# A hybrid encoder layer on one core: even and odd sums in the FNet transform, input statistics from position-major copies, a spread filter network, and a second place for split activations

## Chip, cores and metric

The kernel runs on one core of a Trainium2 chip. The metric is the device time of one execution in microseconds (us); the time of a kernel is the median of its runs.

## What is computed

One layer of an encoder for 512 positions of width 2048. The input is normalised and projected; the columns of the projection feed four groups of 1024 channels and a gate. Each group has its own mixer, each result is RMS-normalised per group, multiplied by the SiLU of its gate, and a last product brings the 4096 channels back to 2048. The reference, cut:

```python
h = rms_norm(x, pre_g);  proj = h @ w_in
a, f, hy, q, gate = split(proj)
u = a_val * sigmoid(a_gate)                              # group A: convolution of 31 taps,
y_a = silu(layer_norm(depthwise_conv(u))) @ conv_pw_w + b  # layer norm, pointwise product
y_b = fft2(f).real @ fnet_w + fnet_b                     # group B: Fourier mixing
y_c = two gated long convolutions of hy                  # group C: Hyena; the filters come from
                                                         # a small network of sines over positions
y_m = attention(q, mem_n @ wk, mem_n @ wv)               # group M: 256 memory tokens
y = rms_norm(each group) * silu(gate)
out = x + rms_norm(y @ w_out, post_g)
```

## The kernel before

All numbers are float32. A product in full precision is made of three fast ones: `split` (L77 to L83) writes the rounded high part of a tile on ACT and the rest on DVE, and `mm3` (L111 to L114) multiplies high by high, low by high and high by low. A weight tile of 128x1024 arrives by one DMA on SP's queue (`load`, 3 buffers `raw`), is split (`wsplit`, 3 buffers `wh` and `wl`), and is consumed by TensorE (PE). `project` (L313) is one output tile of the big projection: 16 steps of 3 matmuls of 512 columns, 48 in all, into a PSUM tile `pf`. A generator that is given to it as `fill` is advanced four times within it.

The order in which the instructions stand on each engine is made by a scheduler from the program; it pulls splits and loads ahead of where they are written. Each engine, and SP's queue of DMAs, then runs its own list strictly in order.

The stages, in order of time:

- **Values loop** (L291 to L310): 16 steps, each loads a slice of `wv`, and every second step a pair of memory slices. Beside it, eight pairs of `xT`, the channel-major input, arrive; ACT squares them and the memory slices, and POOL adds the squares up in `xacc` and `macc` (L189 to L207).
- **Norm of the input**: 8 products with a column of ones (`column_sums`, L156) sum `xacc` over the partitions; `spread` (L147) brings the 512 factors to all partitions by four small products.
- **Keys loop** (L346 to L352): 16 steps with `wk`, matmuls of 256 columns; beside it the normalised input is formed and split into `hH` and `hL`.
- **Filter network** (L257 to L289), after the first of four early query projections: two matmuls (L273, L280) with a sine between them that takes DVE several steps.
- **Filters, then the Hyena group** with the first convolutions. The change does not touch them.
- **FNet group**: a product with `w_f` (folded over positions), then products with a cosine table `cg` and a sine table `sg` (L727 to L752) of 512 columns, small products with `cgx` (L740 to L744), the transform along positions, and `out_product` (L790 to L834), which runs as `fill` of projections.
- **Attention**, with gates and convolutions.
- **Layer norm of group A** (L941 to L973): the mean is subtracted (L952), the squares are summed in `vacc` by ACT and POOL (`group_square`, L480), then column sums, root, spread, and per channel tile a scaling, a SiLU and a split into `uH` and `uL`. Projections for the last gates run on PE meanwhile.
- **Pointwise product of group A**, its last gates, then `group_norm(0, ...)` (L503): column sums, spread, and for seven tiles a scaling (L500) and the product with an early gate (L998).
- **Last product** (rounds of L1027 on): 5 rounds over 32 slices of the mixed channels, group C first, then B, M and A. Activations are split into `jh` and `jl` (3 buffers each) in pool `wp4`, which is opened when the memory of pool `wp5` (`uH`, `uL`, `lnt`, and the early gates that reuse `uL`) has been given back, so it waits for the last reader of that memory.

## Time and profile before

| what | value |
|---|---|
| median of 3 runs | 1719.39 us (1713.63 to 1721.88) |
| profiled execution | 1716.29 us |
| its span, first to last instruction | 1714.5 us |
| PE busy | 1655.3 us, 97% |
| DVE busy | 1221.9 us, 71% |
| ACT busy | 813.6 us, 47% |
| POOL busy | 189.9 us, 11% |
| mean granted clock of TensorE | 0.987 of full speed |
| moved by DMA | 240.27 MB, mean 140 GB/s |

PE's busy share overlaps neighbouring matmuls, so it is read as where PE has work, not as speed. A matmul's row gives its length, some of which overlaps the next one; the pace is the length of a stretch without idle time over the count of matmuls in it. Names of tiles stand without buffer numbers. `<-` after a wait names what ended it.

### The profile page before, as it was taken

How to read it: one execution, taken by the hardware profiler on the slowest of the kernel's cores; microseconds unless marked ns; L12 is line 12 of the kernel's file. 1: busy time of each engine (PE TensorE's matmuls, PEld its weight loads, DVE VectorE, ACT ScalarE, POOL GpSimd, SP SyncE). 2: the span in 40 equal slices, each digit the busy share in tenths (PEclk: the TensorE clock that was granted, in tenths of full speed). 3: DMA queues.
4: the chain of work that ended last, by engine and by line, in shares of the span. 5: the costliest groups of instructions: out<-in, count | busy, mean ns of one | idle time of the engine just before them, and what ended most of it. 6: DMA issues, size and time to landing. Idle time of an engine off the chain costs nothing.

```text
span 1714.5 us, 21887 instructions
## 1 busy us (share of the span) xinstructions
PE 1655.3 (97%) x8201; PEld 1386.6 (81%) x8201; DVE 1221.9 (71%) x1835; ACT 813.6 (47%) x1185; POOL 189.9 (11%) x146
## 2 busy tenths in 40 slices
PE   7999999999999999999999999999999699999997
PEld 5997888887777778878888888888878588888876
DVE  7866987378797887989874979985562545454586
ACT  6645655344343443424344355445454434444564
POOL 5101422011020120100000020100212000000000
PEclk9999999999999999999999999999999899999999
DMA  8654545768576684623434334232123523222355
GB/s 290 227 185 156 160 139 158 218 155 176 136 171 150 146 181 126 137 93 106 134 105 133 105 124 153 81 111 86 62 98 109 193 98 102 93 101 98 128 203 179
DMA packets 87487, 240.27 MB, mean 140 GB/s; under 512 B 8915, under 2 KB 26579, under 8 KB 86869
## 3 DMA queue, kind: packets, MB, share of 16 engines
q1 hardware_dynamic: 80468, 213.70, 38.6%
q0 software_dynamic: 6912, 25.17, 7.9%
q8 instruction: 64, 1.05, 0.2%
q14 instruction: 43, 0.34, 0.1%
HBM read 220.21 MB, written 18.63 MB: 139 GB/s over the span
## 4 chain that ended last, share of the span: by engine, by line
PE 78%; DVE 14%; DMA 2%; issue 2%; ACT 2%; POOL 1%; SPq 0%; DVEq 0%; ACTq 0%; POOLq 0%
PE pf L114 14%; PE pf L112 14%; PE pf L113 14%; PE pg L113 11%; PE pg L112 11%; PE pg L114 11%; DVE y L525 5%; DVE wl L80 2%; DVE yc L629 1%; DMA raw<-in_wv_dram 1%; POOL vacc L485 1%; ACT wh L79 1%; DMA wl<-in_w_std_dram 1%; DVE y L630 1%; DVE pq L568 1%
## 5 line engine op out<-in xcount | busy, mean ns | idle before, releaser
L112 PE MATMUL pf<-hH,wh 128*128 128x512 f32 x1280 | 505.6, 395 | 0.0
L114 PE MATMUL pf<-hH,wl 128*128 128x512 f32 x1280 | 502.7, 393 | 0.3 <-DMA wl<-in_w_std_dram 0.3
L113 PE MATMUL pf<-hL,wh 128*128 128x512 f32 x1280 | 502.1, 392 | 0.0
L80 DVE TENSOR_TENSOR wl<-raw,wh 128x1024 fp32r<-128x1024 f32 (+1 forms) x240 | 304.0, 1269 | 151.6 <-ACT wh L79 151.0
L79 ACT ACTIVATE wh<-raw 128x1024 fp32r<-128x1024 f32 (+1 forms) x240 | 247.5, 1033 | 231.3 <-PE pf L113 140.8
L114 PEld LDWEIGHTS pf<-hH,wl 128*128 128x128 f32 x1280 | 241.5, 189 | 49.6 <-DMA wl<-in_w_std_dram 0.7
L113 PEld LDWEIGHTS pf<-hL,wh 128*128 128x128 f32 x1280 | 241.9, 189 | 46.9 <-issue 0.2
L112 PEld LDWEIGHTS pf<-hH,wh 128*128 128x128 f32 x1280 | 241.7, 189 | 46.9 <-issue 0.5
L80 DVE TENSOR_TENSOR jl<-y,jh 128x512 fp32r<-128x512 f32 (+1 forms) x154 | 91.3, 597 | 121.6 <-ACT jh L79 120.5
L79 ACT ACTIVATE jh<-y 128x512 fp32r<-128x512 f32 (+1 forms) x154 | 84.4, 550 | 178.6 <-PE pg L113 113.4
L112 PE MATMUL pg<-wh,jh 128*128 128x512 f32 x384 | 150.6, 392 | 11.2 <-ACT jh L79 11.2
L113 PE MATMUL pg<-wl,jh 128*128 128x512 f32 x384 | 150.5, 392 | 0.0
L114 PE MATMUL pg<-wh,jl 128*128 128x512 f32 x384 | 150.4, 392 | 0.0
L107 ACT ACTIVATE wh<-raw 128x1024 fp32r<-128x1024 f32 x48 | 51.0, 1061 | 99.8 <-PE pf L113 51.8
L525 DVE SCALAR_TENSOR_TENSOR y<-ubuf,par,y 128x512 f32<-128x512 f32 x120 | 93.0, 775 | 3.5 <-ACT y L523 1.5
L112 PEld LDWEIGHTS pg<-wh,jh 128*128 128x128 f32 x384 | 72.8, 189 | 26.6 <-ACT jh L79 11.5
L114 PEld LDWEIGHTS pg<-wh,jl 128*128 128x128 f32 x384 | 72.6, 189 | 15.2 <-DVE jl L80 0.2
L113 PEld LDWEIGHTS pg<-wl,jh 128*128 128x128 f32 x384 | 72.7, 189 | 15.1
L108 POOL DMA_DIRECT2D wl<-in_w_std_dram x48 | 41.7, 870 | 286.2 <-ACT wl L106 274.3
L106 ACT ACTIVATE wl<-raw 128x1024 fp32r<-128x1024 f32 x48 | 50.2, 1046 | 0.0
L525 DVE SCALAR_TENSOR_TENSOR y<-ub,par,y 128x512 f32<-128x512 f32 x60 | 46.4, 773 | 2.3 <-ACT y L523 1.1
L1016 POOL TENSOR_TENSOR xres<-xres,og 128x512 f32<-128x512 f32 x4 | 6.7, 1682 | 372.2 <-ACT og L1015 372.2
(380 smaller groups left out, 2916.8 us busy)
## 6 DMA issues: line engine op xcount, KB each, us to landing
raw<-in_w_std_dram SPq DMA_DIRECT2D x160, 512.0 KB, 4.2
raw<-in_wo_dram SPq DMA_DIRECT2D x77, 512.0 KB, 3.3
wl<-in_w_std_dram POOLq DMA_DIRECT2D x48, 512.0 KB, 7.8
raw<-in_wk_dram SPq DMA_DIRECT2D x16, 512.0 KB, 4.0
kd<-y SPq DMA_DIRECT2D x16, 512.0 KB, 4.9
y<-kd SPq DMA_DIRECT2D x32, 256.0 KB, 6.0
raw<-in_w_f_dram SPq DMA_DIRECT2D x16, 512.0 KB, 3.2
raw<-in_wv_dram SPq DMA_DIRECT2D x15, 512.0 KB, 5.2
```

Source lines behind the costliest of these rows:

```text
L79: act.activation(h, src, AF.Copy)
L80: dve.tensor_tensor(l, src, h, op=sub)
L106: act.activation(l, raw, AF.Copy, scale=-1.0)
L107: act.activation(h, raw, AF.Copy)
L108: pool.dma_start(l, src, accum_op=add)
L112: pe.matmul(ps, wh, xh, start=start, stop=False)
L113: pe.matmul(ps, wh, xl, start=False, stop=False)
L114: pe.matmul(ps, wl, xh, start=False, stop=stop)
L485: pool.tensor_tensor(acc, sqt, acc, op=add)
L525: dve.scalar_tensor_tensor(o, u[:, t:t + L], conv_w[:, ct, t:t + 1], o, op0=mul, op1=add)
L568: dve.tensor_tensor(pq[:, 0], z0, z1, op=add)
L629: dve.scalar_tensor_tensor(yv, pcv[:, h], cinv[:, o, ct:ct + 1], yv, op0=mul, op1=add)
```

## The change

Six edits.

1. **Start.** 24 products of a tile of ones with itself are put ahead of all other work on PE.
2. **Input statistics.** The sums of squares come from position-major copies: `squares` loads 128 positions (1 MB) and one ACT instruction squares and sums them into a column of `sums`. Four loads of `x` stand in the values loop (steps 5, 8, 10, 12), two of `mem` in the keys loop (steps 8, 11). The loads of `xT` move to the keys loop. The squares and POOL sums of before, and the column sums with ones, go.
3. **Filter network.** It becomes a generator that the four early query projections advance, with four empty steps ahead of each of its first two matmuls.
4. **FNet.** The columns of `w_f` are reordered into even and odd ones, so that a table of 256 columns serves for both halves of the result; the halves are put together by sums and differences (`both`) after the product. The matmuls with `cg` and `sg` have 256 columns each, in the same number; those with `cgx` fall from 30 to 18. One row of the folded output weights is now loaded by its own DMA (`fw0`).
5. **Layer norm and statistics of group A.** The sums of squares move from POOL to DVE; the squares go to PSUM tiles, or to the tile `stat` that also holds mean and root in turn.
6. **Last product.** `jh` and `jl` get a pool of their own, `wj` (2 buffers each), which is opened before `wp5`. In round 0 they come from there alone; in later rounds every third comes from a single buffer in `wp4`. Scaling and gating of group A becomes a generator that round 0 advances in its weight steps 2 to 11; `wp5` is closed and `wp4` opened at weight step 12. The load of `post_g` moves to step 12 of each round.

```diff
+    pw = pf()
+    for _ in range(WARM):
+        pe.matmul(pw[:, 0:P], ones, ones, start=True, stop=True)
...
+    def squares(src, m, j):
+        t = wt("xp", (P, 2048), bufs=2)
+        sp.dma_start(t, src[P * m:P * m + P, :])
+        act.activation(t, t, AF.Square, accum_out=sums[:, j:j + 1])
...
-    XAT = {0: 0, 2: 1, 4: 2, 5: 3, 7: 4, 9: 5, 10: 6, 12: 7}
+    XAT = {5: 0, 8: 1, 10: 2, 12: 3}
...
         if k in XAT:
-            x_square(XAT[k], x_)
+            squares(a["x"], XAT[k], XAT[k])
...
-    pn = pf()
-    column_sums(pn, xacc[:, 0:512], 4, True, False)
-    column_sums(pn, xacc[:, 512:1024], 4, False, True)
-    spread(rs, rstd_of(pn[:, 0:4], 4, 1.0 / D), 4, pf)
+    spread(rs, rstd_of(sums[:, 0:4], 4, 1.0 / D), 4, pf)
...
         raw = load(a["wk"][k])
+        if k % 2 == 0:
+            sp.dma_start(xts[k // 4][:, k % 4:k % 4 + 2, :], a["xT"][:, k:k + 2, :])
         mem_keys(k, raw)
+        if k in (8, 11):
+            squares(a["mem"], k % 8 // 3, 4 + k % 8 // 3)
...
-    project_early(1)
-    filter_net()
-    project_early(3)
+    net = filter_net()
+    next(net)
+    project_early(4, net)
+    for _ in net:
+        pass
...
+    cgH, cgL = wload(a["cg"][:, 0:1024])
+    for c in (0, 1, 4, 2, 3):
+        h = c // 2 % 2
+        v = slice(256 * h, 256 * h + 256)
         for n in range(3):
             if c < 4:
-                mm3(psT[n], eeH[:, c, s], eeL[:, c, s], th, tl, c == 0, False)
+                w_ = slice(256 * c, 256 * c + 256)
+                mm3(psT[n][:, v], eeH[:, c, s], eeL[:, c, s], cgH[:, w_], cgL[:, w_], c % 2 == 0, c == 3)
...
+    def both(ps, odd_first):
+        o_ = wt("odd", (P, 256), bufs=1)
+        act.activation(o_, ps[:, 256:512], AF.Copy)
+        t = wt("bth", bufs=1)
+        dve.tensor_tensor(t[:, 0:256], ps[:, 0:256], o_, op=add)
...
                 if k == 0:
-                    act.activation(we[0:1, :], raw[0:1, 0:512], AF.Copy)
+                    sp.dma_start(we[0:1, :], a["fw0"][hf:hf + 1, :])
...
         dve.tensor_tensor(y, y, mean, op=sub)
-        group_square(y, vacc, lnt[:, 2 + ct % 2, :], ct == 0)
+        sq = vacc if ct == 0 else pg()
+        act.activation(sq, y, AF.Square)
+        if ct:
+            dve.tensor_tensor(vacc, sq, vacc, op=add)
...
+    def finish_conformer():
+        spread(rsg[0], rstA, 4, pf)
+        for ct in range(CT):
+            group_scale(0, ct, yA)
+            if ct < EARLY:
+                y = yA[ct // 4][:, ct % 4, :]
+                dve.tensor_tensor(y, y, gA[:, ct, :], op=mul)
+            yield
...
+            if r == 0 and 2 <= kp < 12:
+                next(conformer, None)
+            if r == 0 and kp == 12:
+                w5.close()
...
-                jh = wt("jh", dt=F32R, bufs=3)
-                jl = wt("jl", dt=F32R, bufs=3)
+                jp, nb = (wj, 2) if r == 0 or n % 3 else (wp, 1)
+                jh, jl = (jp.tile([P, 512], F32R, tag=t, name=nm(t), bufs=nb) for t in ("jh", "jl"))
```

How the lists of instructions move is shown at three places. The first is SP's queue of DMAs at the start of the keys loop, before (`raw` takes a slice of `wk`, `vdm` stores a piece of the finished values):

```order
L87 DMA raw_633<-in_wk_dram 128x1024
L87 DMA raw_667<-in_wk_dram 128x1024
L234 DMA vdm<-mst_549 128x512
L234 DMA vdm<-mst_552 128x512
L87 DMA raw_701<-in_wk_dram 128x1024
L234 DMA vdm<-mst_555 128x512
L87 DMA raw_735<-in_wk_dram 128x1024
```

And now, a little later in the same loop (`y` takes a pair of `xT`, `xp` 128 rows of `mem`):

```order
L92 DMA raw_747<-in_wk_dram 128x1024
L342 DMA y_2_81<-in_xT_dram 128x1024
L92 DMA raw_782<-in_wk_dram 128x1024
L92 DMA raw_816<-in_wk_dram 128x1024
L342 DMA y_3_82<-in_xT_dram 128x1024
L200 DMA xp_847<-in_mem_dram 128x2048
L92 DMA raw_854<-in_wk_dram 128x1024
```

A load of `xT` stands after every second slice of `wk`, and two loads of 1 MB between them.

The second is DVE in the layer norm of group A, before (`lnt` holds the mean, `rsg` the factors of group M, `wl` is the low part of a gate's weights):

```order
L952 TENSOR_TENSOR y_526_3004<-y_526_3004,lnt_10854 128x512 x3
L952 TENSOR_TENSOR y_527_3005<-y_527_3005,lnt_10854 128x512 x4
L500 SCALAR_TENSOR_TENSOR y_1710_10131<-y_1710_10131,par,rsg_10823 128x512
L80 TENSOR_TENSOR wl_10983<-raw_10980,wh_10982 128x1024
L500 SCALAR_TENSOR_TENSOR y_1710_10131<-y_1710_10131,par,rsg_10823 128x512
```

And now (`stat` holds the mean, each `pg` a tile of squares):

```order
L976 TENSOR_TENSOR vacc<-pg_10844,vacc 128x512
L972 TENSOR_TENSOR y_516_2989<-y_516_2989,stat_10824 128x512
L976 TENSOR_TENSOR vacc<-pg_10848,vacc 128x512
L496 SCALAR_TENSOR_TENSOR y_1691_10096<-y_1691_10096,par,rsg_10788 128x512
L976 TENSOR_TENSOR vacc<-pg_10852,vacc 128x512
L654 TENSOR_TENSOR y_1691_10096<-y_1691_10096,sgt_10920 128x512
L976 TENSOR_TENSOR vacc<-pg_10856,vacc 128x512
L85 TENSOR_TENSOR wl_10958<-raw_10955,wh_10957 128x1024
```

All seven sums now stand ahead of the low part `wl` of the gate's second weight tile.

The third is PE at the passage to the last product, before (`gaccA` is the sum of squares of group A):

```order
L114 MATMUL pf_11487<-hH,wl_11521 128x512
L158 MATMUL pg_11552<-ones,gaccA 128x1 x4
L153 MATMUL pg_11560<-diag_11561,ones 128x128
L153 MATMUL pg_11560<-diag_11564,ones 128x128
L153 MATMUL pg_11560<-diag_11567,ones 128x128
L153 MATMUL pg_11560<-diag_11570,ones 128x128
L112 MATMUL pg_11600<-wh_11608,jh_11612 128x512
```

And now, at the passage, and where the factors of group A are spread:

```order
L119 MATMUL pf_11462<-hH,wl_11496 128x512
L167 MATMUL pf_11527<-ones,gaccA 128x1 x4
L117 MATMUL pg_11542<-wh_11548,jh_11552 128x512
L118 MATMUL pg_11542<-wl_11549,jh_11552 128x512
```

```order
L119 MATMUL pg_11545<-wh_11586,jl_11607 128x512
L162 MATMUL pf_11622<-diag_11623,ones 128x128
L162 MATMUL pf_11622<-diag_11626,ones 128x128
L117 MATMUL pg_11542<-wh_11640,jh_11644 128x512
```

The spread stands 48 matmuls later, behind the first four slices; on DVE the low parts of the first two slices, `jl_11553` and `jl_11569`, stand ahead of the layer norm.

## Rows read from the trace of the kernel before

**Rows 1.** The page, part 2: granted clock of TensorE in 40 slices, in tenths.
```profile
PEclk9999999999999999999999999999999899999999
```

**Rows 2.** Waits of PE: who waited for whom, us in total, times, longest.
```profile
PE pg L112 <- ACT jh L79: 11.2, 1, 11.2
...
PE pg L113 <- DVE wl L80: 5.1, 4, 3.4
...
PE pg L158 <- POOL vacc L485: 3.5, 1, 3.5
PE pg L153 <- DVE diag L152: 3.2, 3, 2.7
PE pg L273 <- ACT mb L251: 2.7, 1, 2.7
```

**Rows 3.** Windows: length, busy us (instructions) by engine, granted clock, DMA share, GB/s.
```profile
20.00:30.00 10.00, 9.12 (x39) 6.86 (x39) 9.43 (x6) 8.31 (x12) 9.22 (x4) 1.00 0.90 344
63.00:109.00 46.00, 46.00 (x384) 45.88 (x384) 39.28 (x50) 28.63 (x37) 0.00 (x0) 1.00 0.60 203
125.00:140.00 15.00, 12.29 (x45) 8.98 (x44) 9.16 (x14) 5.26 (x7) 0.00 (x0) 0.89 0.23 78
899.00:921.00 22.00, 22.00 (x107) 18.41 (x106) 11.24 (x21) 10.83 (x24) 0.00 (x0) 0.92 0.44 136
1230.00:1260.00 30.00, 26.50 (x113) 21.70 (x112) 20.78 (x28) 14.01 (x20) 13.17 (x7) 0.89 0.18 60
1260.00:1330.00 70.00, 70.00 (x311) 58.00 (x310) 28.04 (x32) 35.12 (x50) 10.26 (x7) 1.00 0.33 109
1330.00:1360.00 30.00, 15.93 (x65) 12.81 (x64) 18.52 (x33) 11.90 (x22) 0.54 (x1) 0.72 0.59 228
```

**Rows 4.** Timeline of PE: start us, length us, line, operation, count [idle before].
```profile
6.16 0.80 PE L112 MATMUL pg<-wh,y 128*128 128x512 f32 x1 [6.16 <-ACT wh L79]
...
62.70 0.61 PE L153 MATMUL pf<-diag,ones 128*128 128x128 f32 x4
63.07 0.36 PE L112 MATMUL pg<-y,wh 128*128 128x256 f32 x1
...
1339.67 0.98 PE L153 MATMUL pg<-diag,ones 128*128 128x128 f32 x4 [0.16 <-DVE diag L152]
```

**Rows 5.** Groups of instructions, DVE, 12 to 60 us: count | busy us, mean ns.
```profile
L80 DVE TENSOR_TENSOR wl<-raw,wh 128x1024 fp32r<-128x1024 f32 x16 | 29.6, 1877 | 4.6 <-ACT wh L79 4.5
```

**Rows 6.** The same, DVE, 64 to 106 us.
```profile
L80 DVE TENSOR_TENSOR wl<-raw,wh 128x1024 fp32r<-128x1024 f32 x15 | 18.4, 1224 | 4.9 <-ACT wh L79 4.9
```

**Rows 7.** The same, ACT, 0 to 106 us.
```profile
L206 ACT ACTIVATE sq<-y 128x1024 f32<-128x1024 f32 x7 | 7.4, 1056 | 0.7 <-DMA y<-in_xT_dram 0.6
```

**Rows 8.** Tile cgxH: its instructions, duration, first and last start us.
```profile
L744 PE MATMUL pg<-cgxH,eeL x15: 250/251/251, 909.4 to 912.5; 128*128 128x2 f32 x15
```

**Rows 9.** Timeline of PE, filter network.
```profile
130.42 1.12 PE L273 MATMUL pg<-mb,fwp 128*128 128x512 f32 x2 [2.71 <-ACT mb L251]
```

**Rows 10.** Tile ft: a DVE operation that reads PSUM.
```profile
L425 DVE TENSOR_TENSOR ft<-pg,ex x32: 674/682/693, 161.5 to 287.2; 128x512 f32<-128x512 f32 x32
```

**Rows 11.** DMA issues: count, KB each, median us to landing.
```profile
raw<-in_sg_dram SPq DMA_DIRECT2D x4, 256.0 KB, 2.6
```

**Rows 12.** Tile vacc: its instructions.
```profile
L485 POOL TENSOR_TENSOR vacc<-lnt,vacc x7: 1260/1620/3967, 1236.8 to 1249.7; 128x512 f32<-128x512 f32 x7
```

**Rows 13.** Timeline of DVE, layer norm.
```profile
1235.35 4.30 DVE L952 TENSOR_TENSOR y<-y,lnt 128x512 f32<-128x512 f32 x7
```

**Rows 14.** Groups of instructions, DVE, 1340 to 1352 us.
```profile
L500 DVE SCALAR_TENSOR_TENSOR y<-y,par,rsg 128x512 f32<-128x512 f32 x8 | 5.6, 748 | 1.5 <-ACT rsg L154 1.5
```

**Rows 15.** Groups of instructions, 1357 to 1440 us (round 0 of the last product).
```profile
L80 DVE TENSOR_TENSOR jl<-y,jh 128x512 fp32r<-128x512 f32 x31 | 21.5, 693 | 40.6 <-ACT jh L79 40.0 <-PE pg L113 0.5
L79 ACT ACTIVATE jh<-y 128x512 fp32r<-128x512 f32 x31 | 19.6, 632 | 50.8 <-PE pg L113 50.8
...
L79 ACT ACTIVATE wh<-raw 128x1024 fp32r<-128x1024 f32 x15 | 15.7, 1044 | 0.0
```

More of the change, by code (lines that the diff above doesn't have):

```diff
@@ L172, in encoder_kernel @@
     memL = [ytile(i, F32R).rearrange("p a (c n) -> p (a c) n", c=2) for i in (2, 3)]
-    xacc = wt("xacc", (P, 1024), bufs=1)
-    macc = wt("macc", bufs=1)
+    sums = cst.tile([P, 8], F32, tag="sums", name="sums")
     def mem_parts(k):
@@ L271, in filter_net @@
         dve.tensor_scalar(feat[32:33], posf[32:33], 1.0 / L, None, op0=mul)
+        for _ in range(4):
+            yield
         ps = pg()
@@ L278, in filter_net @@
         sine(h1[:64], arg[:64], 64)
+        for _ in range(4):
+            yield
         ps = pg()
@@ L729, in encoder_kernel @@
     psX = pg()
-    for c in range(5):
-        raw = load(a["cg"][c], 512)
-        th, tl = wsplit(raw[:, 0:512])
+    cgH, cgL = wload(a["cg"][:, 0:1024])
+    raw = load(a["cg"][:, 1024:1280], 256)
+    caH, caL = wsplit(raw[:, 0:256], 256)
+    for c in (0, 1, 4, 2, 3):
+        h = c // 2 % 2
+        v = slice(256 * h, 256 * h + 256)
         for n in range(3):
@@ L760, in encoder_kernel @@
     for n in range(2):
-        split(toH[:, n, :], toL[:, n, :], psS[n])
+        split(toH[:, n, :], toL[:, n, :], both(psS[n], True))
     gate(2, 6, yC)
@@ L1125, in _arrange @@
     r["x"] = v["x"][0]
+    r["mem"] = v["mem"][0]
     r["xT"] = v["x"][0].T.reshape(KD, P, L).transpose(1, 0, 2)
```

118 lines of the change are left out of this document (57 added, 61 removed).

## Prediction

> **What bounds the kernel now.** I read the page first: PE is busy for 97% of the span, and the clock is granted in full but for one slice [rows 1]. So a stage is as long as its matmuls, plus what PE waits, plus what it loses at the low clock. The windows give the pace. From 1260 to 1330 us PE never rests, and 311 matmuls of 512 columns take 70 us: 0.225 us each; in the keys loop 384 matmuls of 256 columns take 46 us: 0.120 us each [rows 3]. Half the columns is thus nearly half the time. Then the waits of PE, each with its place: 11.2 us for `jh` and 2.7 for a `diag` at the passage to the last product, 5.1 for low parts `wl`, 3.5 for `vacc`, 2.7 for the filter network's `mb` [rows 2]. Behind a wait the clock falls to its lower level, 1.2 GHz instead of 2.4: a window of length T with mean clock c has (1-c)T/0.5 us at it, and PE loses half of those in which it works. That is 3.3 us at the low level in the filter network, 3.5 in the FNet transform, 6.6 in the layer norm, 16.8 at the passage [rows 3]. What PE does without waiting is the floor; every edit but the FNet one is aimed at time above it.
>
> The sum is made against the profiled execution, 1716.3 us (span 1714.5 and 1.8 around it). The median is 3.1 us above it, inside the spread of its runs, 8 us.
>
> **Start and values loop.** The first matmul runs at 6.16 us, the first of the keys loop at 63.07 [rows 4]. Between lie 192 matmuls, 192 x 0.225 = 43.2 us; 56.9 passed, so 13.7 were lost. Three things go. First, the first 12 matmuls run at the low level and lose 12 x 0.225 = 2.7 us. The dummies take that over but have a price of their own: a small f32 product shows as two instructions, four take 0.61 us at the full clock and 0.98 at the low one [rows 4], so 24 products take 7 to 12 us from about 1 us on. I take an end at 9, since the clock rises on the way: the first real matmul comes 2.8 us later and the two cancel. Second, POOL. While it sums squares (9.2 of 10 us busy at 20 to 30 us [rows 3]) the DVE split of a weight tile takes 1.88 us [rows 5]; in the keys loop, with POOL still, the same one takes 1.22 [rows 6]. Sixteen of them give back 10 us to a DVE that was full (9.4 of 10 [rows 3]), and PE's waits for `wl` go. ACT's squares cost the same: 4 of 2048 columns, by 1.06 us for 1024 [rows 7] 2.1 each. Third, the 16 instructions of the column sums. What is late next is the DMA: 14.9 MB as before (`x` takes the place of `xT`), at the best rate of this trace, 344 GB/s, 43.3 us against 43.2 of matmuls. I leave 3 us of waits (0 to 7) and 0.5 for the spread: 9 + 43.2 + 3.5 = 55.7. **Gain 7.4 us** (3 to 11).
>
> **Keys loop.** It has no loss now: 46.0 us for 384 matmuls, DVE 39.3 busy, DMA at 203 GB/s [rows 3]. Added are `xT` (4.2 MB) and `mem` (2.1 MB); with `wk` (8.4) and `vdm` (1.0) that is 15.7 MB, at 344 GB/s 45.6 us: just what PE takes. A late load of `xT` also holds the `wk` slices behind it on SP's queue, and through DVE's strict order the next `wl`. Three buffers cover some; I take 2 us of waits (0 to 7), less 0.9 for the eight instructions of column sums of `macc` that go, by 0.11 each [rows 8]. **Loss 1 us.** The Trainium skill, *DMA: Bandwidth & Descriptors*, section Measured (HBM→SBUF, 128 partitions, SWDGE, issued from GpSimd), gives 425 GB/s for a large stream of a core alone; by it the loop's bytes would take an estimated 37 us, no wait would be left, and the sum would be 2 us lower. This trace never shows over 344, so I keep to the row.
>
> **Filter network.** PE stands 2.71 us at L273 [rows 9] and loses half of 3.3 us at the low clock behind it, 4.4 in all. L273 now stands 11 matmuls later (2.5 us) and the wait nearly closes. L280 gets only 4 more matmuls of cover, while two splits of 512 columns and a `wl` come in between on DVE, 2 x 0.61 + 1.22 = 2.4 us by [rows 6]; I leave 1.1 us of waits. **Gain 3.3** (1 to 4.4).
>
> **FNet.** 42 matmuls with `cg` and 24 with `sg` go from 512 to 256 columns: 66 x (0.225 - 0.120) = 6.9 us. Of the tiny ones 12 go: fifteen of every other one start between 909.4 and 912.5 us [rows 8], 0.111 each, so 1.3 us. The rest no longer stand in one block, and I expect the low clock behind them (3.5 us, 1.8 lost) to go. `both` adds 5 ACT copies and 10 DVE operations of 256 columns, under 0.68 us each [rows 10], beside 192 matmuls (43 us) of the projections that follow: free, while DVE is half idle there [rows 3]; without that cover up to 7 us. The DMA of one row into the folded weights comes behind a DVE sum and ahead of a split that PE needs. The nearest load lands in 2.6 us [rows 11]; twice that is the upper bound, nothing the lower one, since the row `rx` is already waited for in the same place. I take 1.5 for both. **Gain 8.5** (5 to 10). The Trainium skill, *TensorE: Matmul & The Clock Gate*, section Wait — 56ns, not 53.3ns?, puts the floor from start to start at about 25 ns however few the columns; by it the 12 tiny matmuls would give back an estimated 0.3 us and the sum would be 1 us higher. The row shows 0.111, and the measured pace stands in the sum.
>
> **Layer norm.** Seven POOL sums, median 1.62 us and up to 3.97, start from 1236.8 to 1249.7 us [rows 12], PE waits 3.5 us for the last [rows 2], and of 6.6 us at the low clock half are lost: 6.8 us. On DVE a sum with a PSUM operand takes 0.68 [rows 10]; seven subtractions start at 1235.35 and take 4.30, 0.61 each [rows 13]. After the third of them (1237.2) DVE has 7 sums, 4 subtractions, a scaling of 0.75 and a product like a sum, 7 x 0.68 + 4 x 0.61 + 0.75 + 0.68 = 8.6 us, to the last sum: 1245.8, then `wl` until 1247.0. PE came to the sums at 1247.5 (the wait of 3.5 ends at 1251.0); now 8 matmuls fewer stand ahead of them, so it comes at 1245.7, and needs the late `wl` right behind. The wait is not gone, it becomes one of 1 to 2 us. **Gain 5.6** (3 to 6.8).
>
> **Passage to the last product.** Lost today: 11.2 us for `jh`, 2.7 for `diag` [rows 2], and of 16.8 us at the low clock those not idle, 5.6, by half: 16.7. Now the first slices' splits lie in memory of their own and stand ahead, and the spread comes 48 matmuls (10.8 us) after the column sums. Moved into round 0 are 8 scalings of 0.75 [rows 14] and 7 products, about 11 us of DVE against 54 of matmuls: covered. The 4 loads of `x` keep their place on SP's queue, with five slices of `w_out` ahead of them (27 us of matmuls) against 12 us of transfer at 344 GB/s: covered. Two buffers instead of three let a split start one step (2.7 us) ahead; `jh` and `jl` take 0.63 + 0.69 [rows 15]. I leave 1.7 us of small waits. **Gain 15** (10 to 16.7).
>
> **Sum.** 7.4 - 1 + 3.3 + 8.5 + 5.6 + 15 = 38.8; 1716.3 - 38.8 = 1677.5, **1678 us**. All good ends give 1666, all bad ones 1700.
>
> **Rivals.** (1) *The early loops become bound by transfers*: with `x`, `xT` and `mem` 30.6 MB move in 102 us. Against it: 300 GB/s is below 344. For it: the queue is strict, and the buffers are three. At 290 GB/s the two loops take 105.5 us plus a start of 6, 111 against 109 now: nothing of the 6.4 is left, and up to 8 more is lost: about 1692. (2) *The passage keeps a wait*, because ACT's and DVE's order holds the first `jl` behind the gate's product and root, or the `x` loads delay `w_out` by their 12 us: 1690. (3) *The clock does not do what is hoped*: the dummies end late, and the low stretches stay although the waits shrink: 1.7 + 1.8 + 3.3 us come back, 1685. (4) *Slower*: with two buffers each of the 24 steps of round 0 is as long as its chain on ACT and DVE when all fall on one step, 0.63 + 1.04 + 0.69 + 1.22 + 0.75 + 0.69 = 5.0 us instead of 2.7 [rows 6, 14, 15]; 24 x 2.3 = 55 us, 1733. It decides only once the chain exceeds 2.7 us in every step; but weights come in every second step, and ACT now idles 50.8 us waiting for PE to free `jh` [rows 15], so I give it little.
>
> **How the numbers follow.** My forecast 0.74, (1) 0.12, (2) 0.06, (3) 0.05, (4) 0.03. Below 1664 would need more than every good end, above 1700 leaves rival (4) and the tail of (1): the range is 1664 to 1700, which takes in runs that differ by some us. A difference of 0.5%, 8.6 us, is about what a measurement of this kernel tells from no change; all cases but (4) lie beyond it, and I keep 0.02 for the tail of (1): faster 0.95, same 0.02, slower 0.03.
>
> **What would show it.** Right: the first keys matmul near 56 us with `wl` at 1.2 us throughout; no wait of PE over 2 us at the filter network, in the layer norm and at the passage; a granted clock of 1.0 at all four; some 7 us fewer between the first `cg` matmul and the projection behind the transform. Wrong: PE idle on `raw` or `wl` in the keys loop with DMA above 0.9; `jh` waits in round 0 with ACT or DVE busy; low clock at 910 us or in the layer norm as before.

## The result: 1677.6 us, and the profile after

The changed kernel takes 1677.57 us (median of 4 runs, 1675.61 to 1678.02); the kernel before takes 1718.13 us beside it (1713.63 to 1721.88). The ratio is 0.9763, with an interval from 0.9737 to 0.9788. The profiled execution is one of 1677.6 us with a span of 1675.8 us, 38.7 us below that of before; the forecast's sum was 38.8. That agreement is better than the working deserves: one loss was not foreseen, and three terms that came out larger than forecast made up for it. That the two nearly cancel is luck.

The page of the changed kernel, part 2: POOL's share of busy time and the granted clock of TensorE in 40 slices.

```profile
POOL 0001322001021120200000011100000000000000
PEclk9999999999999999999999999999999999999999
```

The slice of 8 in [rows 1] is gone, and POOL no longer works in the first slices. The waits of PE in the changed kernel (in total, times, longest):

```profile
PE pg L118 <- DVE tL L85: 4.5, 6, 1.3
PE pg L569 <- DVE pq L564: 4.3, 8, 0.6
PE pg L117 <- ACT wh L84: 3.0, 3, 1.7
PE pg L457 <- DVE y L455: 3.0, 1, 3.0
PE pg L269 <- ACT mb L245: 1.9, 1, 1.9
```

Of the waits in [rows 2] those for `jh` and `vacc` have no answer here, the low parts `wl` hold PE up in the values loop for 0.5 us at most, and `mb` went from 2.7 to 1.9. The wait at L457 is new. It is the column sum that ends a filter step, in a stage that the front part calls untouched.

Windows of the changed kernel, columns as in [rows 3]: values loop, keys loop, filter network, the first filter steps, FNet transform, layer norm, the pointwise product, the passage to the last product.

```profile
20.00:30.00 10.00, 9.48 (x43) 7.51 (x42) 5.27 (x8) 7.15 (x10) 0.00 (x0) 1.00 0.97 364
56.00:102.00 46.00, 44.97 (x371) 44.39 (x370) 39.62 (x52) 30.19 (x39) 0.00 (x0) 1.00 0.90 321
118.00:130.00 12.00, 10.14 (x43) 7.77 (x42) 9.54 (x16) 4.68 (x7) 0.00 (x0) 1.00 0.27 90
172.00:183.00 11.00, 8.03 (x31) 6.33 (x30) 11.00 (x19) 7.64 (x13) 1.75 (x2) 0.69 0.43 141
895.00:917.00 22.00, 22.00 (x139) 19.89 (x138) 15.05 (x29) 12.27 (x24) 0.00 (x0) 1.00 0.50 163
1222.00:1236.00 14.00, 14.00 (x69) 11.71 (x68) 13.96 (x24) 8.82 (x12) 0.00 (x0) 1.00 0.20 63
1253.00:1313.00 60.00, 60.00 (x267) 49.67 (x266) 19.99 (x21) 25.25 (x35) 0.00 (x0) 1.00 0.40 136
1311.00:1328.00 17.00, 17.00 (x84) 14.15 (x83) 9.28 (x14) 9.48 (x14) 0.00 (x0) 1.00 0.83 321
```

The clock is 1.00 at all four places that the prediction named, and PE does not rest in the FNet transform, the layer norm and the passage. Only the window at 172 us is bad: PE is busy for 8 of 11 us, the mean clock is 0.69 (so (1-0.69) x 11 / 0.5 = 6.8 us at the low level), and DVE has no idle time at all.

How far each place lies ahead of before is read from the starts of the same matmuls in the two traces:

| first matmul of | before, us | after, us | ahead, us |
|---|---|---|---|
| the values loop | 6.16 | 8.38 | -2.2 |
| the keys loop | 63.07 | 55.71 | 7.4 |
| the early projections | 110.66 | 104.11 | 6.6 |
| the filters (`fwH`) | 160.8 | 151.7 | 9.1 |
| the Hyena stage (`pq`) | 337.8 | 334.6 | 3.2 |
| the FNet table products | 899.2 | 894.8 | 4.4 |
| the transform along positions (`clH`) | 963.4 | 948.7 | 14.7 |
| the sum of the mean (`csum`) | 1230.3 | 1215.7 | 14.6 |
| the column sums of `vacc` | 1251.0 | 1230.8 | 20.1 |
| the pointwise product (`uH`) | 1280.7 | 1259.0 | 21.7 |
| the column sums of `gaccA` | 1335.1 | 1313.4 | 21.7 |
| the sixth slice of round 0 | 1368.0 | 1329.1 | 38.9 |
| round 1 | 1441.4 | 1402.6 | 38.8 |

Five of these starts as rows of the changed kernel's trace (the views of the tiles; the two numbers in front of the semicolon are the first and the last start):

```profile
L416 PE MATMUL pg<-fwH,h2s x32: 390/399/792, 151.7 to 276.3; 128*128 128x512 f32 x32
L569 PE MATMUL pg<-ident,pq x64: 271/273/329, 334.6 to 749.2; 128*128 128x128 f32 x64
L117 PE MATMUL pg<-clH,teH x15: 281/283/285, 948.7 to 956.6; 128*128 128x258 f32 x15
L167 PE MATMUL pg<-ones,vacc x8: 168/250/250, 1230.8 to 1231.5; 128*128 128x1 f32 x8
L117 PE MATMUL pg<-uH,wh x64: 389/389/389, 1259.0 to 1301.9; 128*128 128x512 f32 x64
```

PE's timeline of the changed kernel, where the wait at L457 stands, and at the passage, where 11 us were idle before:

```profile
176.59 0.98 PE L457 MATMUL pg<-ones,y 128*128 128x1 f32 x4 [2.97 <-DVE y L455]
177.44 0.77 PE L416 MATMUL pg<-fwH,h2s 128*128 128x512 f32 x1
...
1313.43 0.95 PE L167 MATMUL pf<-ones,gaccA 128*128 128x1 f32 x8
1314.25 0.47 PE L117 MATMUL pg<-wh,jh 128*128 128x512 f32 x1
```

The first products of round 0 stand right behind the column sums, as the order promised. In the filters a matmul of 512 columns starts at 177.44 and the next 0.57 us later, not 0.23: the clock is low.

So the table has one large step that goes the wrong way (the keys loop's 0.8 us were forecast). Of the 9.1 us gained up to the first filter product, 3.2 are left at the Hyena stage: 5.9 us were given back in a stage that the prediction left out. The experiments ask why, and what each edit is worth.

### The profile page after: what moved, and what is told of

Its sections match the earlier page's. It is cut to its first block, busy times and chain, and to the rows that moved or that the text cites. A ratio compares the mean times of both kernels' runs of the same rounds, so it can differ in the third digit from the quotient of the medians.

```text
span 1675.8 us, 21848 instructions
## 1 busy us (share of the span) xinstructions
PE 1640.0 (98%) x8213; PEld 1376.8 (82%) x8213; DVE 1209.0 (72%) x1855; ACT 811.6 (48%) x1180; POOL 136.2 (8%) x118
## 4 chain that ended last, share of the span: by engine, by line
PE 77%; DVE 14%; DMA 4%; ACT 3%; issue 2%; SPq 0%; POOL 0%; DVEq 0%; ACTq 0%; POOLq 0%
PE pf L119 14%; PE pf L118 14%; PE pf L117 14%; PE pg L118 11%; PE pg L117 10%; PE pg L119 10%; DVE y L521 5%; DVE wl L85 2%; DVE yc L625 1%; DMA xp<-in_x_dram 1%; ACT wh L84 1%; DMA raw<-in_wv_dram 1%; DMA wl<-in_w_std_dram 1%; DVE y L626 1%; DVE pq L564 1%
## 5 line engine op out<-in xcount | busy, mean ns | idle before, releaser
L85 DVE TENSOR_TENSOR wl<-raw,wh 128x1024 fp32r<-128x1024 f32 (+2 forms) x234 | 288.5, 1235 | 132.3 <-ACT wh L84 130.4
L84 ACT ACTIVATE wh<-raw 128x1024 fp32r<-128x1024 f32 (+2 forms) x234 | 244.0, 1045 | 202.9 <-PE pf L118 139.1
L118 PE MATMUL pf<-wl,jh 128*128 128x512 f32 x116 | 45.2, 390 | 1.2 <-DVE wl L85 1.2
```

The lines of the kernel that those rows point to most:

```text
L84: act.activation(h, src, AF.Copy)
L85: dve.tensor_tensor(l, src, h, op=sub)
L118: pe.matmul(ps, wh, xl, start=False, stop=False)
```

## Experiments

Each kernel differs from the changed one as the diff shows; comparisons of stages go by the starts of the same matmuls in two traces. The kernel before took 1715.0, 1715.9, 1716.6 and 1717.0 us (medians) beside the four sets of runs. Starts are read from one profiled execution of each kernel. In the five whose code is the same up to the Hyena stage (the changed one, and those with the old passage, the scalings ahead, the old FNet and the old layer norm) that stage starts between 333.1 and 337.6 us, so the early stages alone move the time by some 4 us. Single stages repeat better: the same five take 182.9 to 184.6 us for the filters.

### The loads of the filter steps in memory of their own

The raw filter weights lie where the filter network's tiles were. Their first load is issued at 144.9 us, 0.1 us after the network's last operation has ended (144.1 + 0.69 us), and PE wants the first product at 151.7. Before, the load went out at 150.1 and the product came at 160.8, so there were 10.7 us in between instead of 6.8.

```diff
+    wv = ...; vxp = ...
+    ws = ctx.enter_context(ExitStack())
+    wr = ws.enter_context(tc.tile_pool(name="wr", bufs=2))
     w0 = ctx.enter_context(ExitStack())
     wp = w0.enter_context(tc.tile_pool(name="wpn", bufs=2))
...
-        rawf = wt("rawf")
+        rawf = wr.tile([P, 512], F32, tag="rawf", name=nm("rawf"))
...
-        adec = wt("adec")
+        adec = wr.tile([P, 512], F32, tag="adec", name=nm("adec"))
```

> Only the two loads of each filter step (raw weights and decay row) get memory that the filter network does not use. Theory A: the 5.9 us that the changed kernel gives back between the first filter product and the Hyena stage come from these loads: their memory is free only when the network's last operation is done (144.8 us), the tensor engine comes to them 6.9 us later where it came 10.7 us later before, VectorE falls behind, the column sum at L457 stands 3.0 us and 6.8 us at the low clock follow. Then the loads start some 10 us earlier, the 3.0 us wait and the low clock at 176 to 183 us go, and the time falls by 4 to 6 us, to 1672 to 1674. Theory B: VectorE alone is too slow for the first two filter steps, because POOL's sums of squares stretch its operations (0.41 to 1.5 us), loads or not. Then the wait at L457 stays at 2 us or more and the time stays at 1676 to 1679.

It takes 1675.45 us (1673.93 to 1676.38), ratio to before 0.9765 (0.9750 to 0.9779). The wait at L457 is gone, and the stage from the first filter product to the first of Hyena is 179.5 us long instead of 182.9. But a wait of 1.5 us for DVE stands right behind (the next step's first product waits for a PSUM bank) with a short stretch at the low clock. Theory A named a cause, and not the only one. The time lies between the ranges of the two theories, and its ratio is not to be told from the changed kernel's; the gain is read from the stage.

### The filter network called as before

```diff
-    net = filter_net()
-    next(net)
-    project_early(4, net)
-    for _ in net:
-        pass
+    project_early(1)
+    for _ in filter_net():
+        pass
+    project_early(3)
```

> The filter network is called as before (in one piece after the first early projection) and the rest stays changed. Theory A: spreading it over the projections is what brought the first filter product 2.6 us nearer (and so the give-back of 5.9 us behind it): the first filter product comes 2 to 3 us later against the projections, the filters stage loses nothing, and the time is 1674 to 1680. Theory B: the scheduler had already put the network's operations between the projections, and the call's place in the source changes nothing: every stage within 0.3 us of the changed kernel, 1677 to 1678.5.

1677.49 us (1675.74 to 1682.04), ratio 0.9781 (0.9762 to 0.9801). Theory B holds in the order: PE's list has the two network products and the first filter product at the same rows as in the changed kernel. The scheduler had put the network between the projections by itself; spreading it in the source does nothing. The forecast gave this edit 3.3 us. It had looked at the right rows of the order, and credited the wrong edit with them; the next run shows which edit they belong to. The stages vary by more than the 0.3 us of theory B: the filters take 181.2 us here.

### The statistics as before

`squares`, its two calls, `sums`, and the place of the `xT` loads are undone, so that POOL adds up the squares of `xT` and `memT` again.

```diff
-    XAT = {5: 0, 8: 1, 10: 2, 12: 3}
+    XAT = {0: 0, 2: 1, 4: 2, 5: 3, 7: 4, 9: 5, 10: 6, 12: 7}
...
-            squares(a["x"], XAT[k], XAT[k])
+            x_square(XAT[k], x_)
...
-    spread(rs, rstd_of(sums[:, 0:4], 4, 1.0 / D), 4, pf)
+    spread(rs, rstd_of(pn[:, 0:4], 4, 1.0 / D), 4, pf)
```

> The input statistics are taken as before (squares of xT and memT summed on POOL, xT loaded in the values loop), dummies and all else stay. Theory A: the values loop's gain of 7.4 us is POOL's: the weight split in the values loop takes 1.88 us again, the first keys product comes 6 to 8 us later, the keys loop gets its 0.8 us back, and the time is 1683 to 1685. Theory B: transfers bound the early loops, POOL only happens to be busy beside them: the first keys product comes less than 3 us later and the split's length does not matter, 1678 to 1680. If the filter network's 2.6 us hang on this edit as well, they add to either.

The groups of DVE from 12 us to the end of the values loop, first in the changed kernel, then in this one:

```profile
L85 DVE TENSOR_TENSOR wl<-raw,wh 128x1024 fp32r<-128x1024 f32 x15 | 18.2, 1224 | 18.7 <-ACT wh L84 18.5
```
```profile
L85 DVE TENSOR_TENSOR wl<-raw,wh 128x1024 fp32r<-128x1024 f32 x16 | 29.7, 1873 | 5.7 <-ACT wh L84 5.7
L88 DVE SCALAR_TENSOR_TENSOR y<-mt,norm_g,y 128x256 fp32r<-128x256 f32 x12 | 14.7, 1265 | 0.0
```

The split takes 1.87 us again, and the first keys product comes at 62.24 us, 6.5 us later: theory A, as [rows 5] and [rows 6] had it. Yet the whole kernel takes 1679.08 us (1678.01 to 1680.34), ratio 0.9787 (0.9772 to 0.9801), only 1.5 us more than the changed one by the medians, where theory A gave 5 to 7. The first filter product is 5.2 us later (156.9) and the first of Hyena 0.3 us later (334.9): the filters stage is 178.0 us long, and the wait at L457 does not occur (one of 1.5 us stands a step later). The early gain of this edit is real, and nearly all of it is what the filters swallow.

The run shows one thing more. Counted from the first early projection, the network's two products stand behind 74 and 104 matmuls here, as in the kernel before; in the changed kernel, and in the one with the old calls, behind 85 and 119. So it is the statistics edit that made the scheduler move the network, and this run undoes both at once, the early arrival and the move. The table in the account of the filters, below, tells them apart.

### No dummies

The loop of dummy products is left out (`WARM = 0`).

> No dummy products at the start. Theory A (the forecast's): they gain nothing by themselves: the first real product comes 2 us earlier, the first dozen run at the low clock and lose 2.7 us, the first keys product within 1 us of the changed kernel's 55.7 us, time 1677 to 1679. Theory B: the early clock is worth more, since the values loop is bound by products throughout: the first keys product 2 us or more later, 1680 or more. Theory C: the loop is bound by transfers, and the dummies only delay: first keys product 2 us earlier, 1675.5.

1679.13 us (1677.72 to 1680.20), ratio 0.9787 (0.9771 to 0.9804). The first real product comes at 6.49 us, the first of the keys loop at 53.75, the first filter product at 151.0, and the filters stage takes 182.8 us, with the wait of 3.0 us at L457. At the keys loop this is theory C, at the end it is not to be told from the changed kernel. A second kernel without dummies (below) had its first keys product at 56.70, while all those with dummies and the new statistics lie between 53.7 and 56.4: the dummies cannot be seen in the early loops at all. Nothing here speaks against the forecast's "the two cancel".

### The passage as before

`finish_conformer`, the pool `wj` and the steps of round 0 are undone; `jh` and `jl` come from `wp4` with three buffers, after the conformer's pool is closed.

```diff
-                jp, nb = (wj, 2) if r == 0 or n % 3 else (wp, 1)
-                jh, jl = (jp.tile(...) for t in ("jh", "jl"))
+                jh = wt("jh", dt=F32R, bufs=3)
+                jl = wt("jl", dt=F32R, bufs=3)
```

> The passage to the last product as before: the conformer's scalings ahead of it, its split activations in the pool that follows the conformer's, three buffers. Theory A: this part gave 15 us as forecast, or the 17.2 us that lie between the last gate product and round 0 in the two traces: the wait of 11 us for jh, one of 2 to 3 us for diag and 14 to 17 us at the low clock return, everything before is unchanged, time 1692 to 1695. Theory B: part of the 17 us came from the early stages (the x loads or the order had moved), then 1686 to 1690.

Waits of PE, rows of this kernel:

```profile
PE pg L117 <- ACT jh L84: 11.2, 1, 11.2
...
PE pg L162 <- DVE diag L161: 3.0, 2, 2.7
```

1697.77 us (1695.63 to 1698.75), ratio 0.9890 (0.9876 to 0.9905). The same 11.2 and 2.7 us as in [rows 2]. From the column sums of `gaccA` to the sixth slice of round 0 it takes 32.6 us, against 15.7 in the changed kernel and 32.9 before: this part is worth 16.9 us, theory A. The rest of the 20 us lies in the early stages (3.0 us up to the Hyena stage), whose code is that of the changed kernel and which vary by that much between executions; by them the time lies above theory A's range.

### Own memory, but the scalings ahead of round 0

```diff
-    conformer = finish_conformer()
+    for _ in finish_conformer():
+        pass
...
-            if r == 0 and 2 <= kp < 12:
-                next(conformer, None)
```

> The own memory for jh and jl stays, but the eight scalings and seven products of the conformer are asked for ahead of round 0 instead of one per step in it. Theory A: memory alone is not enough: VectorE has them (8 x 0.75 + 7 x 0.6 = 10 us) behind the first jl and ahead of the second, one step (2.7 us) covers a part, so the tensor engine waits 6 to 9 us for jl, with the low clock behind it: time 1685 to 1689, and a diag wait of 2 to 3 us may return on top. Theory B: memory was all that jh waited for, and the order matters little: 1677 to 1680.

Waits of PE in this kernel from 1290 to 1400 us, one row in all:

```profile
PE pg L119 <- DVE jl L85: 5.0, 1, 5.0
```

1686.67 us (1683.22 to 1688.70), ratio 0.9825 (0.9810 to 0.9840). The passage takes 22.1 us instead of 15.7, of which 5.0 are the wait and some 1.4 the low clock behind it (0.93 in the 24 us from 1321). That is theory A. Of the 16.9 us the order gives 6.4 and memory of one's own the other 10.5: the wait for memory, once removed, would have become a wait for DVE's list. The profiled execution is the fastest of four; by the medians the two kernels differ by 9.1 us.

### FNet as before

The tables and products with `cg` and `sg` have 512 columns again, `both`, `fw0` and the reordered tables are gone.

```diff
-                mm3(psT[n][:, v], eeH[:, c, s], eeL[:, c, s], cgH[:, w_], cgL[:, w_], c % 2 == 0, c == 3)
+                mm3(psT[n], eeH[:, c, s], eeL[:, c, s], th, tl, c == 0, False)
```

> The FNet transform as before: cg and sg products of 512 columns, no even and odd halves, tables in the old order. Theory A: the stage's 10.3 us are columns and the tiny products, 6.9 + 1.3 us, and 1.8 us of low clock: the dip near 910 us returns with it, time 1686.5 to 1688.5. Theory B: the low clock there was not due to the tiny products standing in one block, and 1.5 us of waits that the forecast subtracted were real: no dip, 1684 to 1686.

The window at the transform in this kernel:

```profile
912.00:922.00 10.00, 10.00 (x39) 8.02 (x38) 7.18 (x12) 5.98 (x10) 0.00 (x0) 0.85 0.46 155
```

1689.81 us (1686.75 to 1691.16), ratio 0.9840 (0.9824 to 0.9857). From the first table product to the first `clH` product it takes 64.2 us, as before, against 53.9 in the changed kernel: 10.3 us. The clock falls again, right behind the thirty tiny products (starts 0.11 us apart from 908.02 us on), though PE has no wait there. Theory A: columns, tiny products and the low stretch make 6.9 + 1.3 + 1.8 = 10.0, and the 1.5 us of waits that the forecast took off are not there. The time lies above theory A's range, since the Hyena stage starts 2.3 us later here. The stage itself repeats: 53.9 to 54.2 us in all twelve kernels with the new transform, 64.2 in both with the old one.

### The layer norm's squares on POOL

The squares of the centred values go through scratch in SBUF to `vacc` on POOL again; the conformer's own squares stay on DVE.

```diff
-        sq = vacc if ct == 0 else pg()
-        act.activation(sq, y, AF.Square)
-        if ct:
-            dve.tensor_tensor(vacc, sq, vacc, op=add)
+        group_square(y, vacc, lsq[ct % 2], ct == 0)
```

> Only the layer norm's squares go back to POOL (scratch in SBUF, sums in vacc on POOL); the conformer's own squares stay on VectorE. Theory A: the vacc wait of 3 to 4 us and the low clock of 6 to 7 us at 1230 us return: time 1683 to 1685. Theory B: the wait was mostly the eight matmuls of column sums and the diag wait that the other edits move, and less than 3 us return: 1678 to 1680.

Its wait of PE from 1215 to 1290 us, and two windows:

```profile
PE pg L167 <- POOL vacc L481: 4.3, 1, 4.3
```
```profile
1230.00:1240.00 10.00, 5.68 (x26) 4.56 (x24) 6.84 (x7) 6.58 (x10) 8.45 (x5) 0.85 0.32 105
1240.00:1250.00 10.00, 10.00 (x42) 8.21 (x42) 6.96 (x14) 5.98 (x8) 0.00 (x0) 0.81 0.29 93
```

1687.32 us (1684.48 to 1689.87), ratio 0.9831 (0.9816 to 0.9845). From the sum of the mean to the pointwise product it takes 50.5 us, against 43.3: 7.1 us, theory A. Its range in us was a little low: the sum of the mean already starts 1.7 us later here (1217.4). This stage repeats as well: 43.3 or 43.4 us in all kernels with the sums on DVE.

### Early loads for the filter network

The network itself starts late: DVE is idle for 2.8 us until the positions land at 116.4 us: their loads go out at 112.4 us only, because their memory belonged to the keys loop. Here positions and weights (3 KB of each partition) get a pool that is opened ahead of that loop.

```diff
+    wq = ctx.enter_context(ExitStack())
+    wqp = wq.enter_context(tc.tile_pool(name="wq", bufs=1))
     w0 = ctx.enter_context(ExitStack())
     wp = w0.enter_context(tc.tile_pool(name="wx", bufs=2))
...
-        fwp = wt("fwp", (P, 2, P), bufs=1)
-        posi = wt("posi", (P, 516), I32, 1)
+        fwp = wqp.tile([P, 2, P], F32, tag="fwp", name="fwp")
+        posi = wqp.tile([P, 516], I32, tag="posi", name="posi")
```

> The positions and the first two weight matrices of the filter network get 3 KB that the keys loop does not use, so that their loads need not wait for the keys loop's last stores; all else as changed. Theory A: the network's late start is what is left: VectorE idles 2.8 us for the positions until 116.4 us, the first network product waits 1.9 us, its result frees the memory of the raw filter weights (144.8 us) 7 us before they are needed, and the wait of 3.0 us at L457 with its low clock follows. With the loads early, the products of the network stand 12 and 17 matmuls further ahead, 92 matmuls instead of 75 lie between its second product and the first filter product, both waits go or fall under 1 us, and the time is 1669 to 1673. Theory B (from the run with own memory for the raw weights, which left 1.5 us of waiting and a low stretch): VectorE and POOL bound the first two filter steps whatever comes early; then the first filter product comes earlier and the stage takes longer by as much, 1675 to 1678.

1674.14 us (1673.04 to 1677.10), ratio 0.9759 (0.9746 to 0.9773). The loads of the positions go out at 90.8 us, those of the raw filter weights at 139.0, 10.3 us ahead of the first filter product (149.2), and the stage takes 178.0 us. Theory A is right on the direction, the wait at L457 falls to 0.4 us, and the network's products stand where it said (behind 73 and 102 matmuls); but the time lies above its range, below theory B's, and a wait of 1.5 us behind the first step and a low stretch stay, so theory B has a share.

### The filters' sums on VectorE, with and without the early loads

Both kernels move the three sums of squares of each filter step from POOL to DVE; the first also has the early loads, the second does not.

```diff
-                pool.tensor_tensor(acc, sq, acc, op=add)
+                dve.tensor_tensor(acc, sq, acc, op=add)
```

> As the kernel with early positions, and the three sums of squares of each filter step go from POOL to VectorE, so that POOL is still in the filters stage. Theory A: VectorE gains, since an operation beside POOL takes up to 1.5 us instead of 0.41 or 0.68, some 3 us in each of the first two steps, and the sums cost it 3 x 0.6: the stage is 1 to 3 us shorter than in the kernel with early positions, or the same if no wait is left there. Theory B: the stretch was mostly VectorE's own order, the sums only add work to an engine that is 0.9 busy there, and the stage gets 2 to 6 us longer.

> The changed kernel with the filters' sums of squares on VectorE alone, the network's loads late as they are. Theory A (POOL's stretch of VectorE's operations is one of two causes): the sums reach L457 earlier, the wait there falls from 3.0 to 1 to 2 us, and the filters stage, 181 to 183 us from the first filter product to the first of the Hyena stage, falls to 178 to 180: time 1674 to 1676. Theory B (the late loads are the only cause): nothing is gained, 1677 to 1679, and what the kernel with both edits gained over the one with early loads was spread between runs.

DVE's groups in the first filter steps, kernel with early loads alone (148 to 178 us), then with the sums on DVE as well (152 to 182 us):

```profile
L85 DVE TENSOR_TENSOR y<-ab,y 128x512 fp32r<-128x512 f32 x8 | 7.0, 898 | 0.0
L424 DVE TENSOR_TENSOR ft<-pg,ex 128x512 f32<-128x512 f32 x10 | 6.5, 679 | 0.0
L428 DVE TENSOR_TENSOR ab<-ft 128x256 f32<-128x256 f32 x10 | 6.3, 634 | 0.0
```
```profile
L85 DVE TENSOR_TENSOR y<-ab,y 128x512 fp32r<-128x512 f32 x10 | 6.6, 683 | 0.0
L424 DVE TENSOR_TENSOR ft<-pg,ex 128x512 f32<-128x512 f32 x10 | 6.4, 681 | 0.0
L435 DVE TENSOR_TENSOR y<-fsq,y 128x512 f32<-128x512 f32 x7 | 4.8, 686 | 0.0
L428 DVE TENSOR_TENSOR ab<-ft 128x256 f32<-128x256 f32 x10 | 4.2, 415 | 0.0
```

The window from 172 to 192 us in the changed kernel, with early loads, and with both (the first filter product comes at 151.7, 149.2 and 153.6 us):

```profile
172.00:192.00 20.00, 17.03 (x71) 13.76 (x70) 20.00 (x35) 15.25 (x25) 6.42 (x5) 0.83 0.41 136
```
```profile
172.00:192.00 20.00, 18.52 (x94) 15.72 (x92) 18.81 (x31) 12.26 (x21) 9.17 (x5) 0.91 0.63 197
```
```profile
172.00:192.00 20.00, 18.90 (x115) 16.58 (x114) 19.61 (x36) 11.59 (x20) 0.30 (x1) 1.00 0.39 130
```

With both edits the kernel takes 1672.88 us (1670.43 to 1673.29), ratio 0.9744 (0.9731 to 0.9757): the lowest ratio here, with the stage at 175.0 us and no low clock in it. With the sums alone it takes 1677.32 us (1671.72 to 1677.79), ratio 0.9754 (0.9734 to 0.9773), stage 178.1 us, the wait at L457 1.6 us (with the first filter product as late, near 154 us, the kernel with the old FNet takes 183.1 us). So each edit alone takes the stage from 182.9 to 178 us, and both take it to 175.0 (177.0 in the last kernel, which has them too, with a stretch at 0.83 of the clock from 175 to 185 us); before it was 177.0. For both edits theory A holds. For the sums alone the stage and the wait are theory A's, but the time is one that theory B gave: two of its five executions took 1672 us and three 1677 to 1678. Their intervals overlap with the changed kernel's (0.9737 to 0.9788); that the two edits together win 4 to 5 us rests on the medians and on the stage.

The last kernel has both edits and no dummies.

> As the kernel with early positions and the sums on VectorE, without the dummy products. Theory A: with no wait of over 1.5 us left in the filters, an earlier start would arrive at the end, but the dummies delay the first real product by 2 us and save 2.7 us at the low clock: within 1.5 us of the kernel with dummies, 1671.5 to 1674.5. Theory B: the values loop is bound by transfers (its first keys product came at 53.75 us without dummies, 54 to 56 with them), so that dummies only cost: 1670.5 to 1671.5.

1672.84 us (1671.99 to 1677.68), ratio 0.9749 (0.9731 to 0.9767); the profiled execution is its slowest, with the first keys product at 56.70 us. Theory A, though the spread of its runs leaves little to read.

## Why the prediction was right, and where it was wrong

**Values loop**, forecast 7.4, measured 7.4. The run with the old statistics undoes the edit as a whole (6.5 us at the keys loop); that POOL is what counts in it rests on the split's duration, 1.87 us beside POOL's sums against 1.22. The Trainium skill, *SBUF — State Buffer*, section SBUF: two separate sides, says that VectorE and GpSimd share one pair of ports under an exclusive lock, which a VectorE operation with two SBUF inputs takes against a GpSimd operation that reads SBUF, and that the loser waits for the other's whole instruction. The traces agree: beside POOL's sums `ab<-ft`, with two SBUF inputs, goes from 415 to 634 ns on average and single ones to 1.5 us, while `ft<-pg,ex`, with one input in PSUM, keeps 679 to 681. The new bound is the transfers, as forecast: DMA is at 0.97 from 20 to 30 us.

The prediction's 344 GB/s was the best of the windows that it had read, and not, as it says, the most that the trace of the kernel before shows. While PE waits for `jh` there, the four loads of `x` and slices of `w_out` give this window:

```profile
1338.00:1348.00 10.00, 1.69 (x8) 1.21 (x8) 7.87 (x17) 0.82 (x2) 0.00 (x0) 0.60 1.01 422
```

The Trainium skill's figure of 425 GB/s (*DMA: Bandwidth & Descriptors*, section Measured (HBM→SBUF, 128 partitions, SWDGE, issued from GpSimd)), which the prediction weighed and set aside, is reached there within 1%. In the early loops of the changed kernel the fullest ten us that were read move 391 GB/s (76 to 86 us).

**Keys loop**, forecast -1, measured -0.8: PE idles 1.0 of 46 us at 321 GB/s. So the term came out right although the rate under it was read too low. In the other kernels with the new statistics the loop takes 47.7 to 51.2 us, against 48.4 in the changed one, and in the slowest PE idles 1.7 us and the clock is 0.97; rival 1's loss of 8 us did not come in any.

**Filter network**, forecast 3.3, measured 2.6 from the first early projection to the first filter product (47.6 us against 50.1). The wait for `mb` is 1.9 us where "nearly closes" was said, and the credit was wrong: the edit to the calls does nothing, the statistics edit moved the products. That the move gains anything is not shown. With the same place of the products eight other kernels take 47.1 to 49.6 us for this stretch, and in four of them the clock between the two products is 0.83 as before (0.81) and not 1.00; the kernel with the old statistics, with the old place, takes 47.1. So the 2.6 us are in part luck, and what gives the rest stays open.

**The filters**, forecast nothing, measured -5.9. This is the step that was wrong. The prediction gave a term to every stage that the diff touches and none to the one behind the early stages. And it read the later place of the network's products only as time won for their waits; the 15 matmuls that the second one gained ahead of it are missing behind it. The load of the filter weights goes out when the network's last operation has ended, so it too comes nearer to the product that needs it (product: first filter product, load ahead: from the issue of the first load to that product; the network's place as counted above):

| kernel | network behind, matmuls | from it to the product, matmuls | product, us | load ahead, us | stage, us |
|---|---|---|---|---|---|
| before | 74, 104 | 90 | 160.8 | 10.7 | 177.0 |
| statistics as before | 74, 104 | 90 | 156.9 | 10.7 | 178.0 |
| early loads for the network | 73, 102 | 92 | 149.2 | 10.3 | 178.0 |
| changed | 85, 119 | 75 | 151.7 | 6.8 | 182.9 |
| network called as before | 85, 119 | 75 | 151.0 | 6.8 | 181.2 |
| sums on DVE alone | 85, 119 | 75 | 154.0 | 6.8 | 178.1 |
| early loads and sums on DVE | 73, 102 | 92 | 153.6 | 10.3 | 175.0 |

With POOL's sums in place the stage's length follows the load's lead, 10.3 to 10.7 us or 6.8, and not the arrival: the kernel with early loads comes first of all to the product and loses 1.0 us to before, not 5.9. So the gains ahead were not lost for being early, but because the order lost 3.4 us of matmuls (15 x 0.225) between the network and the filters. DVE, slowed by POOL, is the second chain: it was so before as well (`ab<-ft` takes 634 ns on average from 160 to 190 us in the kernel before), and with the load late it becomes the wait of 3.0 us and 6.8 us at the low clock. Removing either cause gives 4.8 us or more of the stage back (3.4 in the kernel with memory for the filter loads alone, where the network stays late); removing both gives 7.9 in one kernel and 5.9 in the other.

**FNet**, forecast 8.5, measured 10.3: the mechanism was right, the 1.5 us that were taken off for `both` and the row `fw0` were not lost. The low stretch behind the tiny products went when they were dispersed, and returns with them. The floor of about 25 ns from start to start that the Trainium skill gives (*TensorE: Matmul & The Clock Gate*, section Wait — 56ns, not 53.3ns?) is not what they run at: it is 0.11 us, in the run with the old transform too, so the prediction's choice of the row was right.

**Layer norm**, forecast 5.6, measured 7.0 (1215.7 to 1259.0 against 1230.3 to 1280.7). The last sum starts on DVE at 1229.7 and takes 0.68 us, and PE comes at 1230.8: DVE is ready 0.4 us ahead of it, where the forecast left a wait of 1 to 2 us.

**Passage**, forecast 15, measured 17.2. The 1.7 us of small waits did not occur, and rival 2 fell with them. Two buffers lose nothing: round 0 is 38.9 us ahead at its sixth slice and 38.8 at its end, so rival 4 did not come either. These two groups of round 0 in the changed kernel answer to [rows 15]:

```profile
L85 DVE TENSOR_TENSOR jl<-y,jh 128x512 fp32r<-128x512 f32 x32 | 22.1, 692 | 27.2 <-ACT jh L84 26.7 <-PE pg L118 0.5
```
```profile
L84 ACT ACTIVATE jh<-y 128x512 fp32r<-128x512 f32 x32 | 20.1, 631 | 46.6 <-PE pg L118 44.8 <-DVE y L1031 1.7
```

ACT still idles 44.8 us until PE has freed a `jh`, so it is PE that sets the pace.

In all, the three late terms came out 5.4 us larger (1.8 + 1.4 + 2.2), which nearly hides the 5.9 us of the filters, and 1.1 us between the Hyena stage and FNet cover the 0.7 that the filter network missed. Nothing in the working made these sizes match: the mechanisms of the three late terms are shown, the agreement of the sum is luck. Rival 3, that the clock would not do what was hoped, fell at its three places and appeared at a fourth.

## What to carry to other kernels

When a product moves back in the order, the matmuls that it gains ahead of it are missing behind it: count them on both sides, and ask what the next stage's loads wait for, also where the diff touches nothing. Memory that a later step inherits is an order that no queue shows; a few KB of its own for the first load of a stage can be worth more than a rearranged program. And where a scheduler writes the order, compare the orders with and without an edit before the edit gets a term.

## What was not expected of the hardware

The clock does not go by the length of a wait alone. In the filters the kernel before, from 181 to 191 us, and the kernel with the old statistics, from 177 to 187 us, do the same work with the same wait of 1.5 us for DVE, and the clock falls in the second alone:

```profile
181.00:191.00 10.00, 8.28 (x38) 6.26 (x37) 10.00 (x18) 7.38 (x14) 5.31 (x3) 1.00 0.71 220
```
```profile
177.00:187.00 10.00, 8.28 (x31) 6.09 (x31) 10.00 (x19) 7.37 (x14) 5.30 (x3) 0.83 0.71 220
```

At the filter network a longer wait even does less: with the layer norm's squares on POOL PE waits 2.4 us for `mb` and the clock is 1.00 behind it (125.8 to 134.1 us), with the old FNet it waits 1.9 us and the clock is 0.83 (126.0 to 135.9 us), and the code of the two is the same up to there. These two windows hold the same matmuls, so the low stretch costs 1.6 us, and it can come or stay away in a single execution. What tells the two apart was not tried.

The early loops vary by 2 to 3 us between executions of the same code ahead of them (first keys product from 53.7 to 56.7 us with the new statistics), where the stretch from the pointwise product to the column sums of `gaccA`, without a wait, takes 54.4 us in trace after trace; DMA is at 0.97 of its time there, and the cause was not looked into further.
